# The delta rule's inversion: all four steps issued with the input projections

## The chip, the cores and the metric

The kernel runs on one core of a Trainium2 chip. The metric is the device time of one execution in microseconds, and of several executions the median counts. The profile is one further execution, recorded instruction by instruction. In it, PE is TensorE's matrix multiplication and PEld its loading of weights, DVE is VectorE, ACT is ScalarE, POOL is GpSimd, and SP is SyncE, which here issues most of the transfers.

## What is computed

One layer of an encoder on 1024 tokens of width 1024, in float32:

```python
xn = rmsnorm(h, norm_mix_w)
proj = xn @ w_in
q_a, k_a, v_a, qkv_g, z_g, a_g, b_g = split(proj)
attn = windowed_gqa(q_a, k_a, v_a, band_bias, attn_sink)      # 8 heads of 64, 2 key heads, window 128
gdn = gdn_mixer(qkv_g, z_g, a_g, b_g, ...)                    # 4 heads of 128, two directions
h = h + concat([attn, gdn]) @ w_out
hn = rmsnorm(h, norm_ffn_w)
h = h + square(relu(hn @ w_ffn_in)) @ w_ffn_out
out = rmsnorm(h, norm_final_w)
```

The delta part runs a gated delta rule over chunks, forward and backward. Within a chunk it needs the inverse of a unit lower triangular matrix, and from chunk to chunk it carries a state:

```python
a_mat = where(strict, beta * (k @ k.T) * decay, 0)
t_mat = inverse(eye + a_mat)
...
v_new = u - w @ state            # one step per chunk, in order
o = q_c @ state + qk_c @ v_new
state = state * exp(g_last) + k_c.T @ v_new
```

The reference's chunks have 64 tokens. The kernel uses chunks of 128 tokens: 8 chunks, 4 heads and 2 directions, 64 matrices of 128x128 in all.

## The kernel before, in words

Tokens are held transposed, channels on the partitions. Every large product of float32 numbers is made of three matmuls on a high and a low part of each operand (`mm3`, lines 127 to 129); `split` (lines 122 and 123) makes the two parts, a copy on ACT and a subtraction on POOL. A gemm of the projections (`gemm`) is 8 times three such matmuls on one half of the tokens (512). A pair of weight blocks of 128 columns is used in the order: block 0 on half 0, block 1 on half 0, block 0 on half 1, block 1 on half 1 (`pair`).

Inside `phases` the work is written as generators. `weave` takes the next piece of whichever stream stands lowest by its own count, each `yield` adding its number divided by the stream's rate. So the two numbers at a `run(weave(...))` set how two streams are mixed. What is written earlier has the higher priority. The queues of the engines are then laid out at compile time by a simulated timeline (`schedule_with_timeline_sim=True`, line 1389): on each engine the ready instruction of the highest priority goes next, so something of low priority can come early on an engine that has nothing else. Once laid out, each engine works through its queue in that order.

The stages around the change:

- Projections, first for k and q of the delta part, then the woven stage of lines 1304 and 1305. Its first stream is v (`proj_conv`), z (`proj_z`), and the attention's keys, values and queries (`proj_attn`): 28 gemms, seven weight pairs. Its second stream is the preparation of the delta rule: `prep` makes the chunk matrices and writes them to `atd` and `pd` in HBM, `eliminate` inverts the 32x32 diagonal blocks on DVE, `diag_blocks` turns these blocks into the four matrices `ct` and `ctt` (two per direction), which take the four buffers of the group `sc`, and `invert` follows.
- `invert` (lines 695 to 771) builds the 128x128 inverses from the blocks. One step takes 2 chunks of both directions, 16 matrices. It loads their matrices (line 712, into a `dbl`), clears the results `tt` (line 716), copies the diagonal blocks into them (line 720), and then alternates small matmuls with copies: 32x32 tiles (line 726, copied by 729; lines 736 and 740, used by 745 and 752, with the diagonal blocks copied again by line 750 and the rest cleared by 751), then 64x64 tiles (line 759, copied by 761; line 767, used by 770). `tt` lies in `pg` buffers, but for step 1 of the forward direction in a `wh` and step 2 of it in a `wl` (line 714). `range(4)` would be all the steps, numbered 0 to 3.
- `bias_table` (line 535) reads the attention's bias from HBM into four `pg` buffers.
- The woven stage of lines 1322 to 1324. Its first stream, `output`, is the attention (`attn_scores` with lines 550 to 569, `attn_transpose` with 579 and 581, `attn_value` with 591), the output projection of the attention part (`out_attn`), and of the delta part (`out_all`, which calls `out_gdn`, lines 903 to 921, per chunk, and `out_gemm`, line 883), with the tokens' preparation for the feed-forward part (`tokens_second`). Its second stream has the scans of both directions (`scan`): 8 steps each, whose products are line 805 and whose loads are lines 786, 798 and 800; each step takes two `sc` buffers.
- The feed-forward part, from line 1325 on.

Buffers are shared by tags with a fixed count: 24 of `pg`, 2 of `dbl`, 4 each of `sc` and `wr`, 3 each of `wh` and `wl`, 12 of `pt`, and 4 banks each of `psA` and `psB` in PSUM. A tile waits until a buffer of its tag is free. During the projections 16 of the `pg` hold the tokens, both halves in 8 tiles each.

Of the kernel before, what the change touches and what calls it, by code (L numbers as in the profile page):

```python
# [54 lines left out]
def weave(*streams):  # L55

    live = [[0.0, i, g, w] for i, (g, w) in enumerate(streams)]
    while live:
        s = min(live, key=lambda e: (e[0], e[1]))
        try:  # L60
            v = next(s[2])
            s[0] += v / s[3]
            yield v
        except StopIteration:
            live.remove(s)


def run(gen):
    for _ in gen:
        pass  # L70


def chain(*gens):
    for g in gens:
        yield from g


class Block:
# [1191 lines left out]
    def phases(self):  # L1270
# [11 lines left out]
        for half in range(2):  # L1282
# [5 lines left out]
            else:  # L1288
# [10 lines left out]
        tt = [[None] * 4, [None] * 4]  # L1299
# [2 lines left out]
        self.qs = []  # L1302
        self.wo, self.hnt, self.scanned, self.summed, self.rows = [{}, {}], [None, None], set(), [], {}
        run(weave((chain(self.proj_conv(C_GV, "v"), self.proj_z(), self.proj_attn()), 145.0),
                  (chain(self.prep(), self.eliminate(), self.diag_blocks(), self.invert(tt, (0, 1))), 100.0)))
        self.bias_table()

        self.X = {n: [] for n in ("B11", "B21", "B22", "N1", "T2", "T3", "N4")}
# [2 lines left out]
        def output():  # L1311
            yield from self.attention()
            yield from self.out_attn()
            cols[0], rest[0] = self.columns(self.load_w1(0), 1)
            out = self.out_all(range(NT - 1, -1, -1))
            while len(self.summed) < 4:
                yield next(out)
            yield from weave((out, 20.0), (self.tokens_second(), 9.0))

        w_attn = {3: self.load_wout(0, (0,)), 5: self.load_wout(0, (1,)), 7: self.load_wout(0, (3,))}  # L1320
        w_gdn = {1: self.load_wout(1, (0,)), 2: self.load_wout(1, (1, 2)), 4: self.load_wout(1, (3,))}
        run(weave((output(), 100.0),
                  (chain(self.invert(tt, (2, 3)), self.scan(0, tt[0], w_attn), self.load_wout(0, (2,)),
                         self.scan(1, tt[1], w_gdn)), 95.0)))
        ng = DFF // 256
        self.norm_half(0)
# [66 lines left out]
```

## Time and profile before

| What | us |
|---|---|
| Median of 3 runs | 1246.18 |
| Lowest and highest of them | 1244.01, 1246.87 |
| The profiled execution | 1245.29 |
| Its span, first to last instruction | 1243.6 |
| Mean granted TensorE clock in it | 0.983 |

The span is what the views count from: a time in them is in us from the span's start. Rows of a view name the line, the engine, the operation, the tile written and the tiles read. In the view of waits, a row says which line waited for whom, the sum in us, how often, and the longest. In the timeline, a row has the start, the duration, and in brackets the idle time of the engine ahead of it and who ended it. In the windows view, busy time on each engine stands with the number of instructions in brackets.

By the lines' times in the trace, the last gemm of the projections ends at 326.1 us, steps 0 and 1 of the inversion have their matmuls from 268.1 to 298.2, steps 2 and 3 from 326.5 to 369.2, the first scan product starts at 369.1, and the last ends at 568.

### The profile page before, as it was taken

To read this page: it belongs to the slowest core of one execution; us is meant where nothing else is said; L and a number is where in the kernel's file an instruction comes from. 1 tells how busy PE (TensorE), PEld (TensorE's weight loads), DVE (VectorE), ACT (ScalarE), POOL (GpSimd) and SP (SyncE) were. 2 spreads that over 40 slices of the span, in tenths; PEclk is the share of its full clock that TensorE was granted. 3 is DMA by queue.
4 is the path that set the end of the run, shared out by engine and by line. 5 is a ranking of instruction groups with operands and counts; after the bars stand their busy time and mean duration, and the time that the engine had idled before them with its cause. 6 is when DMAs were issued, how large, how long until landed. Compare 5 with 4: busy or idle time off the path is not lost. (4 is left out here: it accounts for less than half of the span.)

```text
span 1243.6 us, 18468 instructions
## 1 busy us (share of the span) xinstructions
PE 1179.3 (95%) x6482; PEld 962.8 (77%) x6482; DVE 854.0 (69%) x1466; ACT 620.9 (50%) x1347; POOL 574.4 (46%) x486
## 2 busy tenths in 40 slices
PE   6999999899879999997899999999999999999997
PEld 5788877778657778876788888888777888888885
DVE  4677667973378996677654453544579797887976
ACT  6455688354575752125464544545555433444343
POOL 5354312224422334234474535445365655665595
PEclk9999999899889999998999999999999999999999
DMA  6134344524746667222234444344679624434323
GB/s 240 52 117 141 104 167 140 180 81 135 172 145 172 168 220 263 96 83 84 86 120 154 151 153 144 144 158 147 214 263 320 235 84 155 152 133 138 98 89 136
DMA packets 121629, 187.62 MB, mean 151 GB/s; under 512 B 11043, under 2 KB 64416, under 8 KB 121537
## 3 DMA queue, kind: packets, MB, share of 16 engines
q1 hardware_dynamic: 96708, 152.58, 37.2%
q10 hardware_dynamic: 16381, 29.67, 6.2%
q0 software_dynamic: 8448, 4.20, 2.0%
q8 instruction: 51, 0.84, 0.3%
q14 instruction: 41, 0.34, 0.1%
HBM read 122.39 MB, written 63.49 MB: 149 GB/s over the span
## 5 line engine op out<-in xcount | busy, mean ns | idle before, releaser
L127 PE MATMUL psA<-pg,wh 128*128 128x512 f32 x416 | 164.8, 397 | 1.7 <-ACT pt L464 1.7
L129 PE MATMUL psA<-pg,wl 128*128 128x512 f32 x416 | 164.1, 395 | 0.0
L128 PE MATMUL psA<-pg,wh 128*128 128x512 f32 x416 | 163.7, 394 | 0.0
L123 POOL TENSOR_TENSOR wl<-wr,wh 128x512 fp32r<-128x512 f32 x44 | 66.7, 1536 | 159.6 <-ACT wh L122 129.4
L1168 DVE TENSOR_TENSOR pg<-pg 128x512 fp32r<-128x512 f32 x112 | 123.0, 1133 | 17.6 <-ACT pg L1167 17.6
L123 POOL TENSOR_TENSOR wh<-wr,wh 128x512 fp32r<-128x512 f32 x32 | 47.4, 1502 | 129.0 <-ACT wh L122 129.0
L128 PE MATMUL psA<-pg,pg 128*128 128x512 f32 x256 | 99.9, 392 | 0.4 <-POOL pg L123 0.3
L127 PE MATMUL psA<-pg,pg 128*128 128x512 f32 x256 | 99.3, 392 | 0.9 <-DVE pg L1213 0.9
L1085 ACT ACTIVATE pt<-pt 128x512 f32<-128x512 f32 x64 | 40.3, 632 | 119.3 <-DVE pt L1075 119.3
L129 PE MATMUL psA<-pg,pg 128*128 128x512 f32 x256 | 99.7, 390 | 0.0
L123 POOL TENSOR_TENSOR pg<-wr,pg 128x512 fp32r<-128x512 f32 x48 | 73.4, 1560 | 51.5 <-ACT pg L122 51.5
L127 PEld LDWEIGHTS psA<-pg,wh 128*128 128x128 f32 x416 | 78.6, 189 | 19.0 <-ACT pt L464 2.1
L128 PEld LDWEIGHTS psA<-pg,wh 128*128 128x128 f32 x416 | 78.6, 189 | 17.8 <-issue 0.9
L129 PEld LDWEIGHTS psA<-pg,wl 128*128 128x128 f32 x416 | 78.6, 189 | 16.8
L1167 ACT CAST pg<-pg 128x512 fp32r<-128x512 f32 x112 | 67.1, 620 | 40.4 <-DMA pg<-sd 29.3
L128 PE MATMUL psB<-pg,pg 128*128 128x512 f32 x192 | 74.9, 390 | 0.8 <-POOL pg L123 0.7
L129 PE MATMUL psB<-pg,pg 128*128 128x512 f32 x192 | 74.8, 390 | 0.2 <-DVE pg L1168 0.2
L127 PE MATMUL psB<-pg,pg 128*128 128x512 f32 x192 | 74.7, 389 | 0.0
L122 ACT CAST wh<-wr 128x512 fp32r<-128x512 f32 x76 | 43.6, 623 | 50.0 <-PE psA L128 30.0
L1075 DVE TENSOR_TENSOR pt<-psB,pt 128x512 f32<-128x512 f32 x39 | 26.9, 689 | 54.0 <-PE psB L129 29.5
L1075 DVE TENSOR_TENSOR pt<-psA,pt 128x512 f32<-128x512 f32 x39 | 26.8, 689 | 51.8 <-PE psA L129 36.3
L127 PEld LDWEIGHTS psA<-pg,pg 128*128 128x128 f32 x256 | 48.1, 188 | 12.6 <-DVE pg L1213 2.1
(395 smaller groups left out, 3265.3 us busy)
## 6 DMA issues: line engine op xcount, KB each, us to landing
sd<-pt ACTq DMA_DIRECT2D x112, 256.0 KB, 2.1
pg<-sd SPq DMA_DIRECT2D x112, 256.0 KB, 2.9
wr<-in_w_ffn_in SPq DMA_DIRECT2D x32, 512.0 KB, 3.6
wr<-in_w_in SPq DMA_DIRECT2D x22, 512.0 KB, 5.0
pg<-in_x SPq DMA_DIRECT2D x16, 512.0 KB, 6.7
wr<-in_w_ffn_out SPq DMA_DIRECT2D x16, 512.0 KB, 4.7
sc<-kvd SPq DMA_DIRECT2D x14, 512.0 KB, 6.0
kvd<-pt SPq DMA_DIRECT2D x16, 256.0 KB, 2.4
```

The lines of the kernel that those rows point to most:

```text
L122: nc.scalar.copy(out=h, in_=raw)
L123: (eng or nc.gpsimd).tensor_tensor(out=l, in0=raw, in1=h.bitcast(F32), op=ALU.subtract)
L127: nc.tensor.matmul(ps, wh, xh, start=first, stop=False, skip_group_check=onto)
L128: nc.tensor.matmul(ps, wh, xl, start=False, stop=False, skip_group_check=onto)
L129: nc.tensor.matmul(ps, wl, xh, start=False, stop=last, skip_group_check=onto)
L1075: self.nc.vector.tensor_tensor(out=out, in0=in0, in1=in1, op=ALU.add)
L1085: self.nc.scalar.activation(out=c, in_=c, func=AF.Relu)
L1167: nc.scalar.copy(out=s[:, 0], in_=raw)
L1168: v.tensor_tensor(out=s[:, 1], in0=raw, in1=s[:, 0].bitcast(F32), op=ALU.subtract)
```

## The change

Steps 2 and 3 of the inversion move from the head of the scans' stream into the preparation's stream, behind steps 0 and 1. Nothing else is changed: the rates of both weaves stay, and so do the buffers.

```diff
@@ -1302,7 +1302,7 @@
         self.qs = []
         self.wo, self.hnt, self.scanned, self.summed, self.rows = [{}, {}], [None, None], set(), [], {}
         run(weave((chain(self.proj_conv(C_GV, "v"), self.proj_z(), self.proj_attn()), 145.0),
-                  (chain(self.prep(), self.eliminate(), self.diag_blocks(), self.invert(tt, (0, 1))), 100.0)))
+                  (chain(self.prep(), self.eliminate(), self.diag_blocks(), self.invert(tt, range(4))), 100.0)))
         self.bias_table()
 
         self.X = {n: [] for n in ("B11", "B21", "B22", "N1", "T2", "T3", "N4")}
@@ -1320,7 +1320,7 @@
         w_attn = {3: self.load_wout(0, (0,)), 5: self.load_wout(0, (1,)), 7: self.load_wout(0, (3,))}
         w_gdn = {1: self.load_wout(1, (0,)), 2: self.load_wout(1, (1, 2)), 4: self.load_wout(1, (3,))}
         run(weave((output(), 100.0),
-                  (chain(self.invert(tt, (2, 3)), self.scan(0, tt[0], w_attn), self.load_wout(0, (2,)),
+                  (chain(self.scan(0, tt[0], w_attn), self.load_wout(0, (2,)),
                          self.scan(1, tt[1], w_gdn)), 95.0)))
         ng = DFF // 256
         self.norm_half(0)
```

By the weave's counts, the preparation's stream was written out to 0.695 of the projections' stage (69.5 of 100, against 145.6 of 145) and is now written out to 0.843, so that steps 2 and 3 stand between the 20th and the 24th of the 28 gemms. In the later stage the scans' stream loses 14.8 of its 92 counts at the head.

## The prediction

> **What bounds the kernel now.** I read the page first: its busy times, then the stretches around the code that is moved, then what the matrix engine waits for there.
>
> ```profile
> span 1243.6 us, 18468 instructions
> PE 1179.3 (95%) x6482; PEld 962.8 (77%) x6482; DVE 854.0 (69%) x1466; ACT 620.9 (50%) x1347; POOL 574.4 (46%) x486
> ```
>
> PE (TensorE) is busy 95% of the span. The change neither adds nor removes a matmul, so time can only come out of the 64.3 us in which PE is idle (1243.6 less 1179.3) or out of matmuls slowed by a lower clock. The next fence shows where those lie: busy time per stretch, with the granted clock in the third column from the right.
>
> ```profile
> core 0: us, PE busy (x) PEld busy (x) DVE busy (x) ACT busy (x) POOL busy (x), PEclk, DMA share, GB/s
> 298.30:326.10 27.80, 27.80 (x126) 23.09 (x127) 5.43 (x8) 6.82 (x11) 12.18 (x11) 1.00 0.69 186
> 326.10:369.20 43.10, 31.74 (x545) 24.29 (x543) 28.85 (x101) 32.70 (x81) 17.54 (x21) 0.80 0.57 144
> 369.20:460.00 90.80, 85.53 (x610) 68.98 (x611) 83.67 (x275) 58.28 (x168) 28.21 (x26) 1.00 0.65 187
> 460.00:524.00 64.00, 62.82 (x354) 54.09 (x353) 40.95 (x110) 14.52 (x47) 19.52 (x16) 1.00 0.53 190
> 524.00:574.00 50.00, 45.63 (x269) 38.98 (x267) 38.02 (x91) 13.91 (x40) 21.41 (x21) 1.00 0.29 95
> 574.00:622.00 48.00, 38.07 (x189) 31.29 (x190) 32.22 (x48) 23.99 (x47) 22.03 (x24) 0.93 0.22 77
> ```
>
> The stretches are: the last projections; the start of the attention with inversion steps 2 and 3 and no scan yet; attention with the scan; output projection of the attention part with the scan; output of the delta part with the end of the scan; the token transposes. What lies behind 622 the change doesn't touch. The last projections leave PE no idle time at all, while ACT is busy 6.82 and DVE 5.43 of 27.80 us. The stretch behind them is the poorest: 43.10 less 31.74 = **11.4 us of idle PE**, and a clock of 0.80, which over 31.74 busy us is **6.3 us** lost (0.20 x 31.74). From 369.2 on PE is dense again. The waits of PE from 326 to 370, which nearly add up to the idle time:
>
> ```profile
> PE psB L767 <- ACT pt L761: 3.4, 2, 3.3
> PE psA L550 <- DMA pt<-qad: 2.8, 1, 2.8
> PE psA L550 <- DVE nm L552: 1.5, 1, 1.5
> PE psB L759 <- DVE pt L752: 1.4, 2, 0.8
> PE psA L591 <- ACT pt L581: 1.1, 1, 1.1
> PE psA L579 <- DVE wr L569: 0.7, 1, 0.7
> PE psA L579 <- DVE nm L552: 0.3, 1, 0.3
> ```
>
> Lines 759 and 767 are the inversion: 3.4 + 1.4 = 4.8 us. The other five are the attention's start: 2.8 + 1.5 + 1.1 + 0.7 + 0.3 = 6.4 us.
>
> **What the step costs, and what it holds up.** One step of the inversion issues 2 loads on SP, 2 + 2 memsets on POOL, 14 copies on ACT, 8 operations on DVE and four blocks of small matmuls. Groups of steps 2 and 3 inside the poor stretch, on ACT and on DVE (busy us, then the mean in ns):
>
> ```profile
> L720 ACT COPY pg<-sc 32x256 f32<-32x256 f32 x12 | 7.6, 635 | 6.1 <-POOL pg L716 6.0
> L750 ACT COPY pt<-sc 32x256 f32<-32x256 f32 x8 | 5.3, 658 | 0.1
> L761 ACT COPY pt<-psB 128x512 f32<-128x512 f32 x2 | 1.1, 572 | 0.0
> ...
> L745 DVE TENSOR_SCALAR pg<-psB 32x256 f32<-32x256 f32 x6 | 2.5, 418 | 0.3 <-PE psB L740 0.3
> ```
>
> That is 14.0 of ACT's 32.70 us, in the way of the attention's exponentials and copies. On PE, step 0 beside the projections shows what a step costs where PE is full:
>
> ```profile
> 267.58 0.39 PE L128 MATMUL psA<-pg,wh 128*128 128x512 f32 x1
> 267.81 0.39 PE L129 MATMUL psA<-pg,wl 128*128 128x512 f32 x1
> 268.12 1.09 PE L726 MATMUL psB<-sc,dbl 32*32 32x32 f32 x64
> 269.14 0.50 PE L127 MATMUL psA<-pg,wh 128*128 128x512 f32 x1
> ...
> 276.57 0.30 PE L759 MATMUL psB<-pt,dbl 64*64 64x64 f32 x2 [0.30 <-DVE pt L752]
> 277.78 1.11 PE L759 MATMUL psB<-pt,dbl 64*64 64x64 f32 x30 [0.92 <-POOL pg L490]
> 279.57 1.15 PE L767 MATMUL psB<-pg,pt 64*64 64x64 f32 x32 [0.68 <-ACT pt L761]
> ...
> 297.10 0.27 PE L767 MATMUL psB<-wh,pt 64*64 64x64 f32 x1 [0.68 <-ACT pt L761]
> ```
>
> Its matmuls take 1.09 + 0.30 + 1.11 + 1.15 us and some 1.2 for lines 736 and 740 (96 records at the pitch of line 726's 64), 4.9 in all, and steps 0 and 1 together left PE idle 0.30 + 0.92 + 0.68 + 0.68 = **2.6 us**. The matmuls of steps 2 and 3 are paid in either place: the projections end some 10 us later, and the stretch behind them has 10 us less to do.
>
> What is held up is the scan. Its chunk buffers come from the group of four `sc`, and the four are the diagonal blocks' matrices (lines 689 to 692), which steps 2 and 3 still read:
>
> ```profile
> L740 PE MATMUL psB<-pt,sc x128: 205/226/269, 273.9 to 361.4; 32*32 32x32 f32 x128
> ...
> 360.17 1.24 SPq L798 DMA_DIRECT2D sc<-kvd  x1
> ...
> 368.02 1.15 PE L767 MATMUL psB<-pg,pt 64*64 64x64 f32 x32 [0.15 <-ACT pt L761]
> 369.10 1.16 PE L805 MATMUL psB<-sc,pg 128*128 128x128 f32 x8
> ```
>
> The scan's first load goes out at 360.2, when step 3 is nearly through them, and its first product follows at 369.1, 43 us after the last projection. With all four steps beside the projections the matrices come free near the projections' end, at some 330, and the scan can start at about 336 to 340, beside the first scores.
>
> **Buffers and queues that the step is moved past.** The tiles `tt` of steps 2 and 3 take three `pg` buffers and one `wl`. Of 24 `pg`, the normalized tokens hold 16, the keys and values 5, steps 0 and 1 three: all are taken until the last gemm on the first token half ends.
>
> ```profile
> L716 POOL MEMSET pg<- x6: 955/956/972, 146.4 to 335.7; 128x1024 f32 x6
> L535 SPq DMA_DIRECT2D pg<-biasd x16: 371/426/1352, 317.3 to 332.6; - x16
> ```
>
> The bias table, the next taker of `pg`, gets its first buffer at 317.3. So the first half of the moved steps (lines 726 to 761, which need no `tt`) can run from 298, and what writes `tt` (lines 716, 720, 745, 770) only in the last 10 us of the projections. That limits the move, it doesn't undo it. The `wl` buffer leaves the projections' weights two of three; they have had two of three `wh` since step 1, and the halves of a weight are taken together, so I cost it at nothing; uncovered, at two later weight pairs, a wait of one split on POOL (1.5 us) each. On SP the moved step's four loads cost nothing: line 712 already issues before 298, as its buffers come free. On POOL the memsets pass the queries' loads (line 600): four at 0.96 us beside 12.18 busy of 27.80; at worst the 2.8 us wait of line 550 grows by one, 1 us. DVE takes some 7 us (2 steps of 8 operations of 0.42 or more) beside 5.43 of 27.80, ACT some 18 (2 steps of 14 copies, most of 0.65) beside 6.82. ACT's queue is the tight one: a weight pair's first split must be done under one gemm (24 matmuls at the 0.23 us from 267.58 to 267.81, 5.5 us), and behind a run of twelve copies (7.6 us) it could come 2 us late, at two pairs. Steps 0 and 1, with such runs, left PE no more than their 2.6 us idle. Bounds of all this: 0 to 2.6 + 4 = 6.6; I take 2.6, which is measured in the same kind of stretch.
>
> **The sum.** (1) The inversion's own waits in the poor stretch go: -4.8 us. (2) The attention's 6.4 us: with ACT 14 us freer and scan products (8 records in 1.16 us, 40 a step, about 4.6 us) to fill in, between 0 and 6.4 goes. Attention with the scan, from 369.2 on, is dense (5.3 us idle in 90.8), but the wait for the queries' landing (2.8) stays; half, -3.2. (3) The clock: 0 to 6.3 back; the first low stretch follows the queries' wait, so half, -3.2. (4) In the projections +2.6. (5) Late stretches: the scan, ahead now, no longer fills PE between 524 and 574; 0 to +12 (worked out below); I take +1, since PE stays dense while the gemms of line 883 have operands, the row nearest to that being 460 to 524, with 1.2 us idle. Together -7.6. The profiled execution took 1245.3 (span 1243.6 and 1.7 around it), 0.9 under the median 1246.2. 1246.2 - 7.6 = **1239** rounded.
>
> A rule that speaks against it: the Trainium skill's page "TensorEngine Tiling (Array Packing)", section "Key Properties", says that changing the tiling mode drains TensorE. The move puts 16 more changes (4 blocks in and out, twice) among dense gemms; if each cost the 0.16 us between a gemm's 0.39 us and its pitch, that is 2.6 us, estimated, and 1241. The trace doesn't show it: at 268.12 and 269.14 modes change with no idle time noted and the next start before the modelled end.
>
> **The rivals.** *A, the tail (slower).* From 524 the delta part's output goes chunk by chunk (transposes of line 918, four to a chunk, then a gemm), each chunk holding two `wr` while the first feed-forward weights hold the other two:
>
> ```profile
> 523.97 0.60 PE L918 MATMUL psA<-ident,wr 128*128 128x128 f32 x4
> ...
> 535.58 0.47 PE L127 MATMUL psA<-pg,pt 128*128 128x512 f32 x1
> ...
> L805 PE MATMUL psB<-sc,pg 128*128 128x128 f32 x76 | 10.8, 278 | 1.0 <-DVE sc L833 1.0
> L918 PE MATMUL psA<-ident,wr 128*128 128x128 f32 x28 | 4.3, 276 | 1.8 <-DVE wr L915 1.8
> L805 PE MATMUL psB<-sc,pt 128*128 128x128 f32 x28 | 4.3, 274 | 0.0
> L805 PE MATMUL psB<-sc,sc 128*128 128x128 f32 x16 | 2.5, 287 | 1.1 <-DVE sc L823 1.1
> ```
>
> Today 120 scan records fill this stretch (some 13.5 us at 0.113). If the scan is done before the attention's output gemms are, the first of these gemms still comes 11.6 us behind the first transpose (523.97 to 535.58), of which 4.4 are idle now (all of the stretch's) and three chunks' transposes take 2: some 5 us of new idle time. If the chain then keeps its 7.1 us a chunk (seven chunks in 50 us) where PE needs 6.1 (24 matmuls of 0.23 and 0.6 of transposes), that is 7 more: +12 in all. With -8.6 from (1) to (4) that is +3.4: **1250**. It decides once the scan ends before about 524 plus the shift. Against it: without the scan DVE answers faster, and the next chunk starts as soon as `wr` frees. *B, no change:* the `pg` wait pushes what writes `tt` behind the projections, step 3 ends so little sooner that some 4 us are won, and the 2.6 us are paid on top: **1245**. For it the full count of 24; against it that lines 726 to 761 need no `pg`. *C, all back:* the whole 11.4 and 6.3 us, less 2.6: **1231**. Here a rule bears: the page "TensorE: Matmul & The Clock Gate", section "Part 1: The HAM clock gate", drops the clock after an idle window of about 3.4 us, longer than any wait that would be left. The trace's clock of 0.80 with no listed wait over 3.3 us says that shorter ones do it.
>
> **How the numbers follow.** The forecast, 1239 (some 1235 to 1243), has 0.45, C 0.12, B 0.18, A 0.25, a quarter of which may come out within the bound. A measurement of this kernel here tells about 0.2%, 2.5 us, from no change. Faster: 0.45 + 0.12 = 0.57; within: 0.18 + 0.06 = 0.24; slower 0.19. The range goes from just under C to 2 us over A, where projections at their bound would add to it: 1229 to 1252.
>
> **What would show it.** Right: lines 726 to 761 of steps 2 and 3 between 298 and the projections' end; that end near 336 to 339; line 798's first load at 325 to 335 and the first product of line 805 by 342; idle PE in the 43 us behind the projections down from 11.4 to 5 or less, and a clock of 0.9. Wrong: gaps in the gemms at the two weight pairs over 3 us; line 716's `pg` memsets behind the projections' end; or, in the stretch of the delta part's output, more idle time than the 4.4 us of now (524 to 574), ahead of lines 918 and 127.

## The result, and the profile after

The changed kernel takes 1265.55 us (median of 4 runs, 1262.32 to 1267.42) against 1246.53 us for the kernel before, measured beside it: a ratio of 1.0150, with a 95% interval of 1.0123 to 1.0177. It is slower by 19 us, where the forecast was 7 us faster; the range of 1229 to 1252 doesn't hold it. The head of its page:

```profile
span 1265.7 us, 18455 instructions
...
PE 1188.9 (94%) x6482; PEld 970.5 (77%) x6482; DVE 851.7 (67%) x1466; ACT 621.7 (49%) x1347; POOL 575.0 (45%) x486
```

The number of matmuls is the same, 6482. PE's idle time rose from 64.3 to 76.8 us (1265.7 less 1188.9), and its busy time by 9.6 us, though it has no more to do. So 12.5 of the 22.1 us in the span are idle time. Of the 9.6, some 6.5 are the clock: in the stretches in which the trace has it at 0.50, PE is busy 29.6 us before and 42.7 us after, and half of that is lost, 14.8 and 21.3 us. What the other 3 are, the trace doesn't show. The next two fences are the view of stretches, the first of the kernel before (steps 0 and 1 of the inversion), the second of the changed kernel: steps 0 and 1, the last projections with steps 2 and 3, the 43 us behind them, the rest of the attention, the output projection of the attention part, the output of the delta part. The columns are those of the prediction's second fence.

```profile
268.10:298.20 30.10, 27.53 (x526) 22.12 (x525) 10.79 (x22) 21.19 (x36) 11.36 (x11) 1.00 0.31 93
```

```profile
268.70:304.00 35.30, 30.92 (x526) 24.88 (x525) 8.93 (x18) 22.62 (x38) 11.31 (x11) 0.85 0.26 79
304.00:344.10 40.10, 38.42 (x578) 31.24 (x575) 13.65 (x25) 19.50 (x32) 15.29 (x17) 1.00 0.50 135
344.10:387.20 43.10, 31.13 (x219) 27.01 (x219) 33.21 (x129) 23.85 (x72) 14.97 (x15) 0.88 0.90 247
387.20:488.20 101.00, 91.00 (x613) 72.22 (x609) 87.22 (x302) 61.06 (x184) 35.83 (x30) 0.97 0.54 158
488.20:557.70 69.50, 64.15 (x351) 55.48 (x351) 36.79 (x102) 11.77 (x39) 15.12 (x13) 0.98 0.38 134
557.70:605.70 48.00, 38.16 (x181) 31.39 (x179) 25.71 (x39) 15.50 (x33) 20.99 (x22) 0.89 0.29 93
```

Steps 0 and 1 hold the same 526 matmuls and take 35.30 us instead of 30.10. The 43 us behind the projections still have 12.0 us of idle PE (11.4 before), although the small matmuls of steps 2 and 3 are gone from them (545 records before, 219 now), and DMA is busy 0.90 of the time (0.57 before). The attention behind that has 10.0 us idle in 101.0. What PE waited for, first beside the projections (268 to 345 us), then behind them (344 to 388 us):

```profile
PE psB L736 <- ACT pt L729: 2.7, 2, 1.7
PE psB L767 <- ACT pt L761: 2.1, 3, 0.7
PE psB L759 <- ACT pg L488: 0.8, 1, 0.8
PE psB L759 <- DVE pt L752: 0.5, 1, 0.5
...
PE psA L550 <- DMA pt<-qad: 10.1, 1, 10.1
PE psB L805 <- DMA sc<-kvd: 0.7, 1, 0.7
PE psA L579 <- DVE nm L552: 0.6, 1, 0.6
PE psA L591 <- ACT pt L581: 0.5, 1, 0.5
```

The inversion's waits and most of the attention's small ones are gone from the stretch behind the projections, as the change meant, and one wait for the queries' landing, 10.1 us instead of 2.8, has taken their place.

By the lines' times in the trace the span's 22.1 us divide so. The last projection ends at 344.1 instead of 326.1: 9.8 of these 18.0 us are the moved matmuls, **8.2 are loss**. From there to the dense part of the feed-forward (621.8 before, 642.0 after) it takes 297.9 us instead of 295.7, though 9.8 us of matmuls have gone from it: **12.0 are loss**. The last 1.9 lie in the feed-forward part.

Two queues show what the moved step does beside the projections. On ACT (the timeline of the changed kernel: start, busy time, and in brackets the idle time ahead):

```profile
264.20 2.78 ACT L720 COPY pg<-sc 32x256 f32<-32x256 f32 x4
266.99 2.64 ACT L720 COPY wh<-sc 32x256 f32<-32x256 f32 x4
269.64 2.67 ACT L720 COPY wl<-sc 32x256 f32<-32x256 f32 x4
272.33 2.67 ACT L720 COPY pg<-sc 32x256 f32<-32x256 f32 x4
275.02 1.14 ACT L122 CAST wh<-wr 128x512 fp32r<-128x512 f32 x2
276.06 0.36 ACT L729 COPY pt<-psB 128x256 f32<-128x256 f32 x1
```

The four copies into `wl` are step 2's. They are the diagonal blocks, ready as soon as the tile is cleared, and stand ahead of step 0's last four, of a weight's split (line 122) and of the copy (line 729) for which TensorE waits 1.7 us. On DVE, later:

```profile
313.18 0.69 DVE L500 TENSOR_SCALAR pt<-psA 128x512 f32<-128x512 f32 x1
322.75 0.88 DVE L745 TENSOR_SCALAR pg<-psB 32x256 f32<-32x256 f32 x2 [8.88 <-POOL pg L716]
323.66 0.69 DVE L500 TENSOR_SCALAR pt<-psA 128x512 f32<-128x512 f32 x1
...
332.40 1.89 DVE L500 TENSOR_SCALAR pt<-psA 128x512 f32<-128x512 f32 x3
```

Line 745 waits 8.88 us for the clear of line 716, which waits for a `pg` of the tokens, and the queries' evacuation (line 500) stands behind it in the queue; then three evacuations stand behind step 3's. So the queries' way to HBM and back starts later: the second query's load (line 600) goes out at 351.0, 6.9 us behind the last projection (before: at 326.3, 0.2 us behind it), and takes 7.0 us to land instead of 5.1.

### The profile page after: what moved, and what is told of

Same layout as the page of the kernel before. It is cut to its first block, busy times and chain, and to the rows that moved or that the text cites. A ratio compares the mean times of both kernels' runs of the same rounds, so it can differ in the third digit from the quotient of the medians.

```text
span 1265.7 us, 18455 instructions
## 1 busy us (share of the span) xinstructions
PE 1188.9 (94%) x6482; PEld 970.5 (77%) x6482; DVE 851.7 (67%) x1466; ACT 621.7 (49%) x1347; POOL 575.0 (45%) x486
## 5 line engine op out<-in xcount | busy, mean ns | idle before, releaser
L129 PEld LDWEIGHTS psA<-pg,wl 128*128 128x128 f32 x416 | 79.0, 190 | 16.9
L127 PEld LDWEIGHTS psA<-pg,pg 128*128 128x128 f32 x256 | 48.0, 188 | 12.5 <-DVE pg L1213 2.1
```

What stands on the lines that cost most here:

```text
L127: nc.tensor.matmul(ps, wh, xh, start=first, stop=False, skip_group_check=onto)
L129: nc.tensor.matmul(ps, wl, xh, start=False, stop=last, skip_group_check=onto)
```

## The experiments

Theory Q: the loss comes from these queues. Theory S: it comes from the scans, which without steps 2 and 3 at their head run ahead of the attention. Later a theory of buffers (P, the shortage of `pg`) and one of filling (F: the stretch behind the projections was never limited by the inversion) came in. The table has every run beside its own runs of the kernel before; the last column is (ratio - 1) x 1246 us.

| Run | Median us | Ratio to before (95%) | us against before |
|---|---|---|---|
| the change | 1265.6 | 1.0150 (1.0123 to 1.0177) | +18.7 |
| e1_behind | 1266.0 | 1.0157 (1.0140 to 1.0174) | +19.6 |
| e2_step2 | 1252.0 | 1.0046 (1.0033 to 1.0060) | +5.7 |
| e3_diag_late | 1266.8 | 1.0149 (1.0115 to 1.0184) | +18.6 |
| e4_nowl | 1268.4 | 1.0177 (1.0162 to 1.0193) | +22.1 |
| e5_over | 1254.0 | 1.0064 (1.0043 to 1.0085) | +8.0 |
| e6_pause | 1258.6 | 1.0082 (1.0054 to 1.0111) | +10.2 |
| e7_behind_pause | 1261.0 | 1.0103 (1.0072 to 1.0133) | +12.8 |
| e8_no_x | 1265.2 | 1.0136 (1.0106 to 1.0167) | +16.9 |
| e9_clear | 1271.9 | 1.0210 (1.0190 to 1.0230) | +26.2 |
| e10_step2_clear | 1251.8 | 1.0040 (1.0019 to 1.0061) | +5.0 |
| e11_before_over | 1244.8 | 0.9998 (0.9983 to 1.0013) | -0.2 |
| e12_left_out | 1235.8 | 0.9923 (0.9894 to 0.9952) | -9.6 |
| e13_over_pause | 1255.8 | 1.0086 (1.0064 to 1.0109) | +10.7 |
| e14_pg25_after | 1253.7 | 1.0075 (1.0049 to 1.0101) | +9.3 |
| e15_step0 | 1249.3 | 1.0038 (1.0023 to 1.0052) | +4.7 |
| e16_pg25_before | 1239.5 | 0.9952 (0.9935 to 0.9968) | -6.0 |
| e17_gates_after | 1265.1 | 1.0158 (1.0135 to 1.0182) | +19.7 |
| e18_gates_before | 1246.6 | 1.0017 (1.0002 to 1.0033) | +2.1 |

### What the move could win at most

The kernel before, with steps 2 and 3 reduced to the clearing of their matrices:

```diff
         for i in steps:
+            if i >= 2:
+                for d in range(2):
+                    tt[d][i] = self.wl((P, 2, GH, P), F32) if (d, i) == (0, 2) else self.pg((P, 2, GH, P))
+                    nc.gpsimd.memset(tt[d][i].rearrange("p c h x -> p (c h x)"), 0.0)
+                for n in (1.4, 2.4, 1.8, 1.8):
+                    yield n
+                continue
             ns = slice(8 * i, 8 * i + 8)
```

> The kernel before without the work of steps 2 and 3 (no loads, copies, products; their matrices are only cleared, and their place in the weave is kept), so the scan reads zeros for four chunks. Its matmuls are 9.8 us of TensorE. Theory F (filler: the stretch behind the projections is set by the queries' landing and the attention's own chain of DVE and ACT, and the inversion only filled it): 0 to 5 us less, 1241 to 1246, with as much or more idle time in the stretch as before (11.4). If the inversion's matmuls and its own waits set the stretch, as the prediction took it: 12 to 18 us less, 1228 to 1234.

It came out between the two: 9.6 us by the ratio (6.0 to 13.2 by its interval), 10.2 by the medians, and the matmuls left out are 9.8. The view of stretches of this kernel, with the prediction's own bounds, and the waits of PE in the stretch:

```profile
326.10:369.20 43.10, 32.24 (x179) 25.45 (x178) 30.88 (x118) 24.17 (x72) 19.39 (x20) 0.84 0.70 185
```

```profile
PE psA L550 <- DMA pt<-qad: 4.0, 1, 4.0
PE psA L591 <- ACT pt L581: 2.5, 2, 1.8
PE psA L550 <- DVE nm L552: 2.1, 2, 1.6
PE psA L579 <- DVE wr L569: 1.4, 1, 1.4
PE psA L579 <- DVE nm L552: 0.8, 1, 0.8
```

There is no inversion in this stretch and its matrices are free; the scan's first 16 products come at 326.9 to 334.6, the next at 363.1, since its place in the weave is kept. Yet PE is idle 10.9 of the 43.10 us (11.4 before), at a clock of 0.84 (0.80). The idle time was the attention's: the queries' landing and the chain of scores, exponentials and transposes on DVE and ACT. With the inversion gone these same waits are merely no longer hidden behind its blocks; 4.0 + 2.5 + 2.1 + 1.4 + 0.8 is 10.8. Over the whole span the idle time is as good as unchanged, 63.8 us against 64.3. **So, on balance, the inversion cost little there beyond its matmuls**, and these 9.8 us have to run somewhere. By this run the move could win about nothing, at the end of the interval 3.4 us (13.2 less 9.8), and the rest is what it costs.

### Position in the queues, and the scans' lead

Steps 2 and 3 written behind the projections' weave, and step 2 alone beside it:

```diff
-                  (chain(self.prep(), self.eliminate(), self.diag_blocks(), self.invert(tt, range(4))), 100.0)))
+                  (chain(self.prep(), self.eliminate(), self.diag_blocks(), self.invert(tt, (0, 1))), 100.0)))
+        run(self.invert(tt, (2, 3)))
```

```diff
-                  (chain(self.prep(), self.eliminate(), self.diag_blocks(), self.invert(tt, range(4))), 100.0)))
+                  (chain(self.prep(), self.eliminate(), self.diag_blocks(), self.invert(tt, (0, 1, 2))), 100.0)))
...
-                  (chain(self.scan(0, tt[0], w_attn), self.load_wout(0, (2,)),
+                  (chain(self.invert(tt, (3,)), self.scan(0, tt[0], w_attn), self.load_wout(0, (2,)),
```

> Steps 2 and 3 are written behind the whole weave of the projections and ahead of the bias table: not with the attention, as in the change, but with a lower priority than every projection. Theory Q (queues: in the changed kernel the moved steps' copies and clears stand ahead of the weights' splits on ACT and of the queries' evacuation on DVE, ACT and POOL): the stretch of steps 0 and 1 is back at 30 to 31 us (35.3 in the changed kernel), the last projection ends at 326 to 333 (344.1), line 550 waits at most 4 us for the queries (10.1), and the time is 1238 to 1250. Rival S (scan: a scan that runs ahead of the attention takes DVE, ACT and SP from it and brings the loads of x together in one burst): the scan starts as early, at 340 to 350, so the time stays at 1255 to 1266.

> Step 2 alone beside the projections, step 3 at the head of the scans' stream as before. Theory Q: the run of sixteen copies on ACT and the clear that waits for a buffer of the tokens both belong to step 2, so most of the loss stays: stretch of steps 0 and 1 at 34 to 36 us, time 1255 to 1263. If each step costs its share, it is half the loss: 1254 to 1258. Rival S: the scan starts some 10 us later than in the changed kernel, and half of what lies behind 373 us comes back.

In e1_behind the projections are untouched: the last ends at 325.3, and 297.00 to 325.30 has PE busy throughout. It is as slow as the change all the same, which is what S expected and Q excluded (the first scan product came at 354.6, later than S's 340 to 350). But its own new loss is plain as well. With the inversion ahead of the first scores, nothing fills it:

```profile
325.30:354.60 29.30, 16.14 (x465) 14.46 (x465) 14.58 (x45) 12.86 (x32) 10.19 (x14) 0.66 0.86 229
```

PE idles 13.2 us here at a clock of 0.66. Step 2 alone costs 5.7 us, a third of the loss, less than either theory had.

The scans held back by the 14.8 counts that steps 2 and 3 had taken at their head, in the changed kernel and in e1_behind:

```diff
+        def pause():
+            for _ in range(2):
+                for n in (1.4, 2.4, 1.8, 1.8):
+                    yield n
...
-                  (chain(self.scan(0, tt[0], w_attn), self.load_wout(0, (2,)),
+                  (chain(pause(), self.scan(0, tt[0], w_attn), self.load_wout(0, (2,)),
```

> The changed kernel, with the scans' stream held back at its head by the 14.8 counts that steps 2 and 3 had there, so that the scans stand against the attention as in the kernel before; nothing else moves. Theory S (the losses behind the projections come from the scans running ahead of the attention: their loads stand beside the queries', they take buffers and DVE first): of the some 12 us lost behind the projections most comes back, the attention's last value matmul is at 462 to 475 (488.2), no wait for pd over 1 us (5.2), time 1250 to 1257. Theory Q alone (what hurts is the queues in the projections and the late queries): the wait of line 550 stays at 8 to 11 us and the time at 1261 to 1268.

> The kernel of e1_behind (steps 2 and 3 written behind the projections' weave; 1266.0) with the same 14.8 counts ahead of the scans. Theory S: the projections are untouched here and the scans no longer run ahead, so 1245 to 1253. If the scans' being ahead is not the cause, but that the inversion stands ahead of the attention's first scores: 1261 to 1268.

Both gain, 8.5 us (18.7 to 10.2) and 6.8 us (19.6 to 12.8): the scans' lead is a cause. In e6_pause the last value matmul of the attention is at 471 instead of 488 us, and no wait for pd is over 1 us. By the profiled spans, the changed kernel loses 13.9 us behind the projections (12.0 and 1.9) and e6_pause 5.1: its span is 12.3 us longer than before, and 7.2 of these lie in the projections, which end at 343.1. But neither comes back as far as S expected, and e7_behind_pause, at 1261.0, lies at the edge of the other reading. The waits of PE in e6_pause from 343 to 388 us say why:

```profile
PE psA L591 <- ACT pt L581: 7.9, 2, 4.4
PE psA L550 <- DMA pt<-qad: 7.5, 1, 7.5
PE psA L579 <- DVE nm L552: 1.0, 1, 1.0
```

With neither the inversion nor the scan beside them (but for the scan's first 16 products, at 343.4 to 345.7; the next comes at 388.0), the attention's first chunks stand bare: 7.9 us for the copies of line 581 where before it was 1.1. This is theory F again.

### The copies ahead of the weight's split

Three attempts to take step 2's copies out of ACT's run of sixteen: another buffer (e4_nowl), another place in the step (e3_diag_late), a clear that depends on the load (e9_clear, and e10_step2_clear on e2_step2).

```diff
-                mk = {(0, 1): self.wh, (0, 2): self.wl}.get((d, i))
+                mk = {(0, 1): self.wh}.get((d, i))
```

```diff
-            for d in range(2):
-                for q in range(4):
-                    nc.scalar.copy(out=t[d][blk(q), :, blk(q)], in_=ctt[d][blk(q), :, ns].rearrange("p x n -> p n x"))
+            def diagonal():
+                for d in range(2):
+                    for q in range(4):
+                        nc.scalar.copy(out=t[d][blk(q), :, blk(q)], in_=ctt[d][blk(q), :, ns].rearrange("p x n -> p n x"))
+            if i < 2:
+                diagonal()
...
             xs = self.pt((P, 8, 64))
             nc.scalar.copy(out=xs, in_=px)
+            if i >= 2:
+                diagonal()
```

```diff
-                nc.gpsimd.memset(tt[d][i].rearrange("p c h x -> p (c h x)"), 0.0)
+                out = tt[d][i].rearrange("p c h x -> p (c h x)")
+                if (d, i) == (0, 2):
+                    nc.gpsimd.tensor_scalar(out=out, in0=a.rearrange("p c h x -> p (c h x)"), scalar1=0.0, scalar2=None,
+                                            op0=ALU.mult)
+                else:
+                    nc.gpsimd.memset(out, 0.0)
```

> The changed kernel with step 2's forward matrix in a buffer of the group pg, not wl, so that its clear and its diagonal copies can't run ahead of step 0's own. Theory Q: ACT's run is twelve copies again, the stretch of steps 0 and 1 is 30 to 31 us (35.3) and the clock in it 1.00 (0.85), the last projection ends 4 to 6 us sooner (344.1); the wait of line 550 stays near 10; time 1256 to 1261. Rival S, or if the run of copies isn't what delays the stretch: 1263 to 1268.

> The changed kernel with the diagonal copies (line 720) of steps 2 and 3 written behind the copy of line 761, near the end of their step; steps 0 and 1 as they are. If the run of sixteen copies on ACT stretches steps 0 and 1: 30 to 31 us there (35.3), clock 1.00, and the last projection ends at 337 to 341 (344.1). DVE's line 745 still waits for the clear, so line 550 still waits 8 to 11 us for the queries: 1257 to 1262. Theory S: what is won in the projections lets the scan start sooner yet and is half lost again: 1259 to 1265.

> The changed kernel, with the wl of step 2 cleared by a product of its loaded matrix with 0 (POOL) in place of the memset, so that neither this clear nor its four diagonal copies on ACT can run before step 2's load. If the run of sixteen copies ahead of a weight's split is what stretched steps 0 and 1: that stretch 30 to 31 us (35.3) at clock 1.00 (0.85), last projection at 338 to 340 (344.1), time 1258 to 1262. If the time comes from elsewhere: 1264 to 1268.

> Step 2 alone beside the projections (e2_step2: 1252.0) with the same clear as in e9_clear. If the run of copies is most of what that kernel loses: 1245 to 1248, even with the kernel before; otherwise 1250 to 1254.

None of the four wins what it would if the run of copies were the price, and the traces show why. In e4_nowl the stretch of steps 0 and 1 did what was expected (first row of the view of stretches), but the last projections lost as much (46.36 us where the changed kernel has 40.10):

```profile
268.70:298.84 30.14, 27.57 (x526) 22.19 (x526) 9.09 (x19) 20.20 (x34) 11.38 (x11) 1.00 0.29 92
298.84:345.20 46.36, 41.70 (x575) 33.29 (x575) 13.65 (x25) 21.71 (x36) 16.13 (x18) 0.93 0.50 130
```

```profile
316.50 10.40 ACT L720 COPY pg<-sc 32x256 f32<-32x256 f32 x16 [2.35 <-POOL pg L716]
326.93 0.37 ACT L729 COPY pt<-psB 128x256 f32<-128x256 f32 x1
```

In ACT's timeline of e4_nowl the four matrices of steps 2 and 3 now all wait for buffers of the tokens; their sixteen copies come in one run of 10.40 us, step 3's copy of line 729 stands behind it, and TensorE waits 4.6 us for that: the 5.2 us were won and lost 45 us later. In e3_diag_late nothing moved: `wl` is copied at 269.3 (269.6 in the changed kernel). The queues are laid out by what is ready in the simulated timeline, and those copies are ready early wherever they are written. In e9_clear the run is twelve copies, and the layout moved TensorE's queue with it (line 736 is line 741 there):

```profile
268.62 1.09 PE L731 MATMUL psB<-sc,dbl 32*32 32x32 f32 x64
269.64 0.50 PE L127 MATMUL psA<-pg,wh 128*128 128x512 f32 x1
269.97 0.40 PE L128 MATMUL psA<-pg,wh 128*128 128x512 f32 x1
273.56 0.24 PE L741 MATMUL psB<-sc,pt 32*32 32x32 f32 x4 [3.19 <-ACT pt L734]
```

Only two gemm matmuls stand between the two blocks (21 in the changed kernel), so the wait for the copy grew to 3.19 us; and the clear by a product takes 2.78 us on POOL where a memset takes 0.96, ahead of a weight's split. e10_step2_clear has the same wait, 3.2 us, and its time is that of its other reading. The 8.2 us in the projections are therefore read from the trace and were not undone by any run.

### Buffers

Steps 2 and 3 written over the matrices of 0 and 1, in the changed kernel (e5_over), in the one before (e11_before_over), and in the changed one with the pause (e13_over_pause):

```diff
-                tt[d][i] = mk((P, 2, GH, P), F32) if mk else self.pg((P, 2, GH, P))
+                if i == 3:
+                    tt[d][i] = tt[d][1]
+                elif (d, i) == (1, 2):
+                    tt[d][i] = tt[d][0]
+                else:
+                    tt[d][i] = mk((P, 2, GH, P), F32) if mk else self.pg((P, 2, GH, P))
```

> The changed kernel with steps 2 and 3 written over the matrices of steps 0 and 1 (step 2's forward one keeps its wl), so the second half of the inverses is lost and the scan reads the wrong ones; what is issued, computed and loaded is the same, but for three buffers of the group pg that nobody waits for. Theory P (the buffers: the clear of line 716 waits on POOL for a buffer of the tokens, line 745 waits for it on DVE for 8.9 us, and the queries' evacuation stands behind both): no such wait, line 550 waits at most 4 us (10.1), time 1250 to 1257; the stretch of steps 0 and 1 stays at 35. Theory Q without P (copies on ACT are enough to hold the queries up): line 550 waits 6 to 10 us, time 1259 to 1265. Rival S: 1262 to 1268.

> The kernel before with the matrices of steps 2 and 3 written over those of 0 and 1, as in e5_over: three pg buffers more that nobody waits for (the scan reads wrong inverses). If what e5_over won (11.6 us) was the shortage of pg that the change itself makes: 1243 to 1248 here. If the shortage is the kernel's own, with or without the change: 1235 to 1240.

> The changed kernel with the matrices written over (e5_over: 1254.0) and the scans held back by 14.8 counts (e6_pause: 1258.6) at once; the scan reads wrong inverses. If the scans' lead and the shortage of pg are two causes, their gains add up: 11.6 and 7 to 8 off 1265.6, 1245 to 1248. If they are one (the scans that run ahead are what takes the buffers): 1252 to 1256.

The time of e5_over is as P expected, by another way than P said: the clears come at 305 us, no line waits for them, and still line 550 waits 6.0 us, since the evacuations stand behind step 3's operations on DVE. What was won lies in the attention: by the trace PE waits 3.1 us from 389 us to its end, against 10.0 in the changed kernel. In the kernel before, the same three buffers win nothing. And with the pause on top nothing more is won (+10.7 against +8.0): the two gains don't add up, as expected if the lead and the buffers are largely **one cause**. The way from one to the other is argued from the code: a scan that runs ahead takes chunk buffers (line 786) and weights earlier, and the attention's score tiles, the output weights and the rows of x, which share the group `pg`, come later. The rows of x are shown below.

The same without leaving anything out: one buffer more, its room taken from small tiles of the gates, which get slices of one `wr` (the gates' seven tiles `gt` likewise); then the controls with the moved tiles but 24 buffers.

```diff
-        return self.buf("pg", 24, shape, dt)
+        return self.buf("pg", 25, shape, dt)
...
-        zero = self.small((P, NK * 16), bufs=1, tag="zab")
+        own = self.wr((P, 1024))
+        zero = own[:, 768:768 + NK * 16]
...
-        abt = self.small((P, NT, 32), bufs=1, tag="abt")
+        abt = own[:, 0:256].rearrange("p (c x) -> p c x", c=NT)
```

> The changed kernel with 25 buffers of the group pg (the room comes from small tiles of the gates, which take a wr early on instead); nothing is left out. If the shortage of pg is what e5_over removed, one of its three buffers gives a part of the 11.6 us: 1257 to 1263. If it was not the number of buffers: 1264 to 1268.

> The kernel before with 25 buffers of pg, as in e14_pg25_after. By e11_before_over, where three more made no difference: 1243 to 1248.

> The changed kernel with the small tiles of the gates in a wr as in e14_pg25_after, but 24 buffers of pg: the control for the buffer. If the 25th buffer is what won 11.8 us there: 1263 to 1268. If the moved small tiles did it: 1252 to 1257.

> The kernel before with the small tiles of the gates in a wr and 24 buffers of pg. If the 25th buffer is what won 6 us in e16_pg25_before: 1243 to 1248. If the moved small tiles did it: 1237 to 1241.

The controls stay at +19.7 and +2.1, so it is the buffer that wins, and not the moved tiles: 10.4 us on the changed kernel, as much from one buffer as from the three of e5_over, and more than expected. The loads of x, which take eight `pg`, show it in SP's timeline: the kernel before, the changed kernel, e14_pg25_after.

```profile
452.26 0.45 SPq L196 DMA_DIRECT2D pg<-in_x  x1
...
464.61 1.20 SPq L196 DMA_DIRECT2D pg<-in_x  x2
...
475.50 2.84 SPq L196 DMA_DIRECT2D pg<-in_x  x2
...
```

```profile
484.21 4.39 SPq L196 DMA_DIRECT2D pg<-in_x  x8
```

```profile
466.81 4.99 SPq L196 DMA_DIRECT2D pg<-in_x  x6
...
```

In the changed kernel all eight go out at once, 32 us later than the first before (18 us of which are the later end of the projections). That burst was my next suspect, because the scan waits 5.2 us for its pd right behind it:

```diff
-            self.h[c] = self.load_x(c)
+            self.h[c] = self.pg((P, D))
+            self.nc.gpsimd.memset(self.h[c], 0.0)
```

> The changed kernel without the eight loads of x in the output projection of the attention part (4 MB; the eight rows are cleared on POOL in their place, so the residual is left out). If the burst of these loads is what makes the scan wait 5.2 us for pd at 498 us: that wait under 1 us, 5 to 8 us less with the clock, 1257 to 1261. If pd is late for its place in SP's queue or for a buffer: the wait stays over 3 us, and the time at 1262 to 1268.

The wait for pd went, and the time stayed within the interval of the change: 2.3 us of it came back as a wait for DVE (line 824), and the output of the delta part kept its waits. So the burst is a sign of the shortage; a price of its own didn't show.

That e16_pg25_before wins 6 us on the kernel before was not expected; with its control at +2.1 that gain is the buffer's too. It is the one complete version that beats both, 1239.5 us. So what a buffer wins is not the same as what the change loses by a shortage, and the two pairs price that shortage differently: 19.7 - 9.3 against 2.1 + 6.0 leaves 2 us that the 25th buffer wins more on the changed kernel, while the gains of e5_over and e11_before_over differ by 10.5. Either way, with one more buffer in both kernels the change still costs some 15 us (9.3 + 6.0; 14.3 by the medians).

### The other way

Only step 0 beside the projections, steps 1 to 3 at the head of the scans' stream (against the kernel before):

```diff
-                  (chain(self.prep(), self.eliminate(), self.diag_blocks(), self.invert(tt, (0, 1))), 100.0)))
+                  (chain(self.prep(), self.eliminate(), self.diag_blocks(), self.invert(tt, (0,))), 100.0)))
...
-                  (chain(self.invert(tt, (2, 3)), self.scan(0, tt[0], w_attn), self.load_wout(0, (2,)),
+                  (chain(self.invert(tt, (1, 2, 3)), self.scan(0, tt[0], w_attn), self.load_wout(0, (2,)),
```

> The move the other way: only step 0 beside the projections, steps 1, 2 and 3 at the head of the scans' stream. Theory F (the attention's start has room, the projections have none): the projections end some 5 us sooner, and the stretch behind them takes step 1's 4.9 us into its idle time: 1240 to 1247. If the stretch behind the projections has no more room (ACT busy 32.7 of 43.1 us already), or the scan starts too late: 1249 to 1256.

The projections end 1.4 us sooner, not 5, and the time is 4.7 us longer. The longest wait behind them is 7.1 us for the copies of line 581, against 1.1 before, while ACT, with the copies of three steps, is busy 44.0 of the 57.3 us from the last projection to the first scan product. Two steps and two is the best of the divisions that were tried.

## Why the prediction was wrong

**What bounds the kernel.** The reading of the poor stretch was right in its size, 11.4 us idle and a clock of 0.80, and wrong in what it was due to. That TensorE waits for lines 761 and 752 says whose result came last, not that the time would be free without it. (The clock cost a little more than the 6.3 us: in the stretches at 0.50, 332.1 to 335.5, 338.9 to 345.8 and 352.6 to 359.4, PE is busy 14.4 us, and half of that is 7.2.)

**Steps (1), (2) and (3), -11.2 together.** This is where the sign was lost. Removing the work altogether won 9.6 to 10.2 us where its matmuls alone are 9.8 (e12_left_out), so the waits and the clock give some 0.4, or 3.4 at the end of the interval, and not 11.2. Steps (1) and (2) counted as two sums what are alternatives: while TensorE waits for the inversion it isn't seen to wait for the attention. In the changed kernel the 43 us behind the projections have 12.0 us idle, not 5 or less. The clock in them was near the expected 0.9, at 0.88, and it didn't help.

**Step (4), the projections, +2.6 within 0 to 6.6.** It measured +8.2, beyond the bound: 3.5 us more idle time (4.4 + 1.7 in the two stretches against 2.6) and 4.3 us of clock make most of it. The run of copies ahead of a weight's split was named, and its wait was there (1.73 us at one place). What the term lacked is the clock: in this view of the changed kernel it is halved for 10.2 us behind the 1.73 us wait, and of the 8.67 busy us 4.3 are lost.

```profile
279.10:289.30 10.20, 8.67 (x138) 7.35 (x139) 4.48 (x8) 7.47 (x13) 4.02 (x5) 0.50 0.35 113
```

The `wl`, costed at nothing, made it possible: it was cleared early, so its copies could run early. The queries, costed at 1 us at worst on POOL, wait on DVE: the `pg` that limits line 716 was seen, but not that line 745 would hold the evacuations behind it for 8.88 us.

**Step (5), the late stretches, +1 within 0 to +12.** The direction was right and the place wrong. Rival A, the tail, didn't happen: by the same view the output of the delta part up to the feed-forward has 13.8 us idle, against 14.3 before, although the scan is through at 549. The loss lies in the attention, 10.0 us idle in 101.0 where the prediction's row had 5.3 in 90.8, and in the output projection behind it, 5.4 in 69.5 (one wait for pd is 5.2 of it) where the row had 1.2 in 64.0. There the scans' lead costs 7 to 8 us (e6_pause, e7_behind_pause), and the shortage of buffers that the change brings between 2 and 10.5, largely the same microseconds. The prediction counted the 24 `pg` up to the projections' end and no further.

**Milestones.** The scan's first load was expected at 325 to 335 and goes out at 340.1; its first product by 342, and it is at 345.3; the projections' end at 336 to 339, and it is 344.1. So the move did what it says, and B and C are out as well: the case that came true, a scan that starts 24 us sooner and thereby slows the attention beside it, wasn't among the rivals.

**The page rules.** The prediction estimated 2.6 us for the changes of mode that, by "TensorEngine Tiling (Array Packing)" (the Trainium skill, section "Key Properties"), drain TensorE. That much isn't visible: from 304.0 to 344.1 the changed kernel takes 2.4 us more than the 27.9 of before (298.2 to 326.1) and the moved 9.8 together, and 1.7 of these are idle time behind the waits listed above; no run isolates the changes. The rule of "TensorE: Matmul & The Clock Gate" (the Trainium skill, section "Part 1: The HAM clock gate"), a drop after an idle window of about 3.4 us, disagrees with the changed kernel if it is read as one wait: the clock halves at 279.1, and the longest wait ahead of that, beside the projections, is 1.73 us.

**What stays open.** How the 12 us behind the projections divide between the scans' lead and the buffers, since the two remedies don't add up; and whether the 8.2 us in the projections could be had back by an order of ACT's queue set by hand, since every edit here was laid out anew and moved other work too.

## What to carry to other kernels

Before work is moved out of a stretch with idle time, run the kernel with that work left out: if that wins no more than the work itself, the waits belong to something else, and the work was filling them for nothing. Price the place it goes to by its tightest queue and its clock, and follow the shared buffers beyond the place of the move, into the stage where the freed stream then runs ahead. And two waits that end one after the other on the same engine can be alternatives, not a sum.

## What the runs showed of the hardware

In the changed kernel one wait of 1.73 us, over at 276.5, and one of 0.53 lie ahead of the halved clock at 279.1, and it stayed halved for 10.2 us (the row from 279.10 to 289.30): 4.3 us lost, more than the waits of that stretch, 3.7 in all. The profiles agree on this: all eleven kernels with a wait of 1.7 to 3.2 us at this place had the clock halved for 10.2 us behind it. Of the eight with waits of 0.30, 0.92 and 0.68 us there, seven kept it at 1.00. The eighth, e16_pg25_before, had it halved for 6.8 us from 278.0 at the same waits, so the waits alone don't decide it. A tensor_scalar of 128x1024 float32 on POOL took 2.78 us where a memset of that size took 0.96. And 4 MB less of loads in a stretch with DMA busy 1.01 of the time (488.2 to 498.1 in the changed kernel) changed the time by less than the measurement can tell.
